# One list of weight buffers for two stages, a pinned entry to the second FFN, later transposes, and one block's token forms over five steps

## The chip, the cores and the metric

The kernel runs on one core of one Trainium2 chip. The metric is the device time of one execution in microseconds. The kernel before took 2645.22 us in the median of three runs (2639.3, 2645.22 and 2656.01 us). One more execution was recorded by the profiler: it took 2644.05 us, of which 2642.3 us lie between its first and its last instruction (the span). All times of the trace below are microseconds from the start of that span.

## The reference

One transformer layer on 256 latent tokens (LAT) and 256 context tokens (CTX) of width 2048, all in float32:

```
mod_l, mod_c = silu(c) @ w_mod + b_mod, silu(c_ctx) @ w_mod + b_mod      # shifts, scales, gates
xl = half_step_ffn(xl, mod_l, 0, ...);  xc = half_step_ffn(xc, mod_c, 0, ...)   # first FFN, 512 tokens
... token mixing: attention heads and mLSTM heads, one output projection ...
xl = half_step_ffn(xl, mod_l, 6, ...)                                    # second FFN, 256 tokens
return rms_norm(xl, g_final)

def half_step_ffn(x, mod, i, g, w_up, w_down):
    h = adaln(x, g, mod, i)
    a, b = split(h @ w_up, 2)                       # w_up 2048 x 2*5632, w_down 5632 x 2048
    return x + 0.5 * gate * ((silu(a) * b) @ w_down)
```

The inner width of 5632 is cut into 11 blocks of 512. The change lies in the two FFNs; what it touches of the rest is the buffer that every weight load passes through.

## The kernel before, in words

**Three products for one.** A float32 operand is split into a high and a low part of a format that TensorE multiplies fast: ScalarE (ACT) copies the weights into the high part and VectorE (DVE) subtracts to get the low part (`split`, L170 and L171, in halves of 1024 columns; `split_whole`, L140 and L141, 2048 columns at once). Each product is then three matmuls: high by high, low by high, high by low. `mm3` (L192 to L194) issues them in the order of its lines; `high_first` and `low_last` (L154, L155, L160) put the two that need only the high part of the weights first. The split halves live in two rings (`ringhi`, `ringlo`) of four places of 1024 columns, so that splitting can be about two halves-pairs ahead of TensorE (PE) and no further.

**Seven products for eight.** Both FFNs save matmuls by a Winograd-style scheme. Tokens and inner width are halved, four quarters a11, a12, a21, a22 of the tokens and four derived token forms (v, n1, s2, s4, s3) meet weights that are sums of four quarters of the weight block. One block of the first FFN's up product is `quad(n)` (L899): seven entries of `order` (L956), each with two steps q = 0 and 1, so 14 steps, numbered 2m + q. A step of the first FFN is 24 matmuls of 512 columns. The sums of weights are made by the DMA engines: a tile `chain_[q]` is loaded plain at the quad's start, used for a11, then a second quarter is added into it from memory by an accumulating DMA (`accum`, L784, issued by GpSimd (POOL)), used for n1, and so on through s2 and a22. So `chain_[q]` is read in steps 0, 4, 8 and 12 (q = 0) or 1, 5, 9, 13 (q = 1), with an accumulating DMA behind each of the first three reads. The entry a12 uses a plainly loaded tile (`plain`), and s4 and s3 share another one (`ra`, loaded by `loaded`, then accumulated into).

**Which tile holds what.** Plain loads go on the queue of SyncE (SP). `raw_tile()` (L118) takes a 128 x 2048 tile from a pool of three, tag `raw`; the pool hands out whichever of its three places has been given back. The two chain tiles are tiles of their own (L783). At the end of a quad `again(q)` (L939) loads the next quad's first quarter into the same chain tile (L817), so it must wait until the split of step 12 or 13 has read that tile, and it is read two steps later. The first FFN's down product has the same shape: `pair(p)` (L1106), five pairs of blocks, 14 steps each, `again(c)` at L1157 with the load at L1159. The second FFN has seven quads of its own (L2068, 14 steps of 12 matmuls), with chain tiles and an `again` of its own (L2110, load at L2113), and three blocks done plainly.

**Other work beside the quads.** While the quads of the first FFN run, the modulation vectors are summed on DVE, a half row at a time: a load of 512 KB (`sraw`, L292, two buffers, SP queue), then multiply and sum (L263). Each finished result `ca` of a quad (512 columns) waits in a list and is turned by four PE transposes (L893), copied by ACT into `stg` (one buffer, L883) and stored to memory (L884).

**Token forms of a down pair.** The seven token operands of a pair are made from the stored hidden tensors. What is made at which step stands in three tables: `first_plan` for the first pair (the entries from step 7 on are for the second pair), `plan` for the middle pairs and `last_plan` (L1078 to L1080). Each name is an instruction on DVE (`v`, `v2`, `u`, `u2`: one subtraction of 1.2 us) or a split to a place (`n1`, `s4`, `s2`, `s3`, `a22`, `a11`, `a12`: one copy on ACT, L768, and one subtraction on DVE, L769); `raw0` and `raw1` load the next hidden tensors (L759).

**What sets the order.** The framework's scheduler writes each engine's list of instructions ahead of time, from the program's order, the dependencies and a timing model of its own; at run time each engine goes through its list in order. `tc.keep_in_program_order` ties one instruction behind the instruction traced just before it on its engine; the token forms of the down pairs are tied in this way (`pinned`, `sub`, `neg_sub`), most others are not.

**The entry to the second FFN.** The last part of the first hidden block is L1951 to L1962: the product of two PSUM tiles (ACT Silu L1960, DVE multiply L1961) and the split of its result (L1932, L1933). Then the PSUM pools are closed and opened anew (L1966 to L1969), so the first matmuls of the next stage write into banks that L1961 reads. The main loop (L2253 to L2263) runs a plain block's up steps, the quads' steps and the down blocks' steps in turn, and steps the making of the four token forms (`token_forms`, L1998) after each of the first main steps.

**The transposes of the second FFN.** A finished hidden result goes on a list with the count of half-steps so far (`wait_turn`, L2061; `tiles` grows by 1 for a quad's step and by 2 for a step of a plain block). `turned` (L2037) transposes the first one on the list when the count has grown by 3. For a quad's second result the last elementwise steps are c21 (L2101): DVE add L2102, ACT Silu L2103, DVE multiply L2071 (`mul`).

Of the kernel before, what the change touches and what calls it, by code (L numbers as in the profile page):

```python
# [9 lines left out]
F32 = mybir.dt.float32  # L10
# [4 lines left out]
ALU = mybir.AluOpType  # L15
# [4 lines left out]
P = 128  # L20
# [28 lines left out]
FB = 4  # L49
# [12 lines left out]
def tile_layer(ctx: ExitStack, tc: tile.TileContext, I: dict, out: bass.AP):  # L62
# [74 lines left out]
    def split_whole(raw):  # L137

        hi, lo = ring(2)
        nc.scalar.activation(hi, raw, AF.Copy)  # L140
        nc.vector.tensor_tensor(lo, raw, hi.bitcast(F32), op=ALU.subtract)  # L141
        return lambda w: (hi[:, w], lo[:, w])

    def load_whole(src):
# [640 lines left out]
    with pool(name="f1u", bufs=1) as f1u:  # L785
# [27 lines left out]
        def part(n, ab, c):  # L813
            return I["w_up1b"][n - 1, ab, c]

        def first_chain(n, c):
            nc.sync.dma_start(chain_[c], part(n, 0, c))  # L817
# [81 lines left out]
        def quad(n, after=lambda step: None):  # L899
# [36 lines left out]
            def chained(ab, c):  # L936
                return lambda q: accum(chain_[q], part(n, ab, c + q))

            def again(q):  # L939
                if n + 1 < NB:  # L940
                    first_chain(n + 1, q)
                else:
                    nc.sync.dma_start(chain_[q], I["w_dn1"][0, 2 * q])

            def loaded(q):
                ra[q] = raw_tile()
                nc.sync.dma_start(ra[q], part(n, 1, 2 + q))
                return ra[q]

            def plain(q):  # L950
# [126 lines left out]

    first_plan = {0: "v n1", 1: "v2 u s4", 2: "s2 u2", 3: "s3 a22", 4: "raw0 raw1", 7: "a11", 8: "a12", 9: "v n1", 10: "v2 u", 11: "s4", 12: "s2 u2", 13: "s3"}  # L1078
    plan = {0: "a22 raw0", 1: "raw1", 4: "a11", 5: "a12", 6: "v", 7: "n1", 8: "v2 u", 9: "s4", 11: "s2 u2", 13: "s3"}
# [26 lines left out]
    def pair(p):  # L1106
# [44 lines left out]

        def loaded(m, cb):
            raw = raw_tile()
            nc.sync.dma_start(raw, w(m, cb))
            return raw

        def again(c):  # L1157
            if p + 1 < NP:
                nc.sync.dma_start(chain_[c], I["w_dn1"][2 * p + 2, 2 * c])  # L1159

        def b22(c):
            ra[c] = loaded(1, 2 * c + 1)
            return ra[c]
# [7 lines left out]
            ("a11", held, X, True, lambda c: accum(chain_[c], w(0, 2 * c + 1)), c11x),  # L1171
            ("a12", lambda c: loaded(1, 2 * c), Z, True, None, c11z),
# [3 lines left out]
            ("s3", lambda c: ra[c], X, False, None, x3),  # L1176
            ("a22", held, Y, True, again, c21),
        )
# [32 lines left out]
    for p in range(NP):  # L1211
        pair(p)

    def block_products(b, wt, t):
# [707 lines left out]
    with f2x:  # L1922
# [28 lines left out]
        for f in range(NPRE, FB):  # L1951
            pab = []
            for ab in range(2):
                wt = load_split(I["w_up2"][f, ab])
                b = bank()[:, :T]
                for k in range(KT):
                    mm3(b, *wt(slice(k * P, (k + 1) * P)), h2hi[:, k, :T], h2lo[:, k, :T], k == 0, k == KT - 1)
                pab.append(b)
            sa = sab_tile()[:, :T]
            nc.scalar.activation(sa, pab[0], AF.Silu)  # L1960
            nc.vector.tensor_tensor(sa, sa, pab[1], op=ALU.mult)  # L1961
            split_hid(hids[0], f, sa)  # L1962
        hscm.__exit__(None, None, None)
# [34 lines left out]
        def token_forms():  # L1998
# [8 lines left out]

            def difference(v, x, y):
# [10 lines left out]
            v, w = (acc2[:, t, 1024:].rearrange("p (k c) -> p k c", k=8) for t in range(2))  # L2019
            difference(v, a22, a21)  # L2020
            put(n1, v)
# [15 lines left out]
        def turned():  # L2037

            if not turn or turn[0][-1] + 3 > tiles[0]:
                return  # L2040
# [372 lines left out]
```

## Time and profile before

| what | value |
|---|---|
| profiled execution | 2644.05 us, span 2642.3 us, so 1.75 us outside the span |
| median of three runs | 2645.22 us (2639.3 to 2656.01) |
| first FFN: up quads, down pairs | about 144 to 949 us, about 949 to 1338 us |
| second FFN from its first plain block on | from 1982 us to the end |
| mean granted clock of TensorE | 0.996 |
| data moved | 679.94 MB, mean 257 GB/s |

In the profile, PE is TensorE's matmuls and transposes, PEld its weight loads, DVE is VectorE, ACT is ScalarE, POOL is GpSimd, SPq and POOLq are the instruction queues of SyncE and GpSimd, which here issue DMAs. A row of the timeline has the start and the length of one instruction (or of several merged, then xN), its engine, its line, the tile that it writes and the tiles that it reads, and in square brackets how long its engine sat idle before it and what ended that idle time. A row of the waits has the waiting engine and line, the engine and line that ended the wait, the total in microseconds, the number of such waits and the longest. A row of the windows has a stretch of time, its length, the busy time of each engine with the number of instructions, the granted clock of TensorE in that stretch (1.00 is full speed), the busy share of the 16 DMA engines and the rate in GB/s.

### The profile page before, as it was taken

Reading aid. Unit: us, or ns where it says so; the run is one execution under the profiler, and the core shown is the slowest. Engines: PE = TensorE matmul, PEld = TensorE weight load, DVE = VectorE, ACT = ScalarE, POOL = GpSimd, SP = SyncE. Lnnn points to the kernel's source line nnn. Section 1 sums busy time; section 2 is a strip of 40 time slices with the busy share of each in tenths; the row PEclk is TensorE's granted clock in tenths of the full one; section 3 lists DMA queues with packets and bytes.
Section 4 is the critical chain, followed back from the end, with each engine's and each line's share of the span. In section 5 each row is a group of like instructions: output and inputs, shape, how many; then the busy total and the mean of one; then the engine's idle time right before and its main releaser. Section 6 shows DMA issues by size and latency. Waiting matters only on the chain. (4 is left out here: it accounts for less than half of the span.)

```text
span 2642.3 us, 33359 instructions
## 1 busy us (share of the span) xinstructions
PE 2595.9 (98%) x12670; PEld 2148.3 (81%) x12670; DVE 2181.9 (83%) x2817; ACT 1345.2 (51%) x1547; POOL 210.7 (8%) x265
## 2 busy tenths in 40 slices
PE   8999999999999999999999999999999999999998
PEld 5787888888888878888889888877898888888887
DVE  6687888878878778888886979798598888887888
ACT  4354444544444455444454346346476555555554
POOL 0000001100000100010110000111000000000001
PEclk9999999999999999999999999999999999999999
DMA  9979999999999988889985867574568999889886
GB/s 376 343 229 259 257 283 269 271 285 280 271 280 268 276 230 237 221 208 230 231 244 215 315 227 246 207 271 159 175 253 262 294 273 295 259 271 307 285 244 188
DMA packets 136800, 679.94 MB, mean 257 GB/s; under 512 B 14392, under 2 KB 24376, under 8 KB 75840
## 3 DMA queue, kind: packets, MB, share of 16 engines
q1 hardware_dynamic: 108384, 496.92, 50.4%
q0 software_dynamic: 27968, 180.37, 34.8%
q8 instruction: 99, 1.62, 0.2%
q10 hardware_dynamic: 288, 0.52, 0.1%
q14 instruction: 61, 0.50, 0.1%
HBM read 658.82 MB, written 18.94 MB: 256 GB/s over the span
## 5 line engine op out<-in xcount | busy, mean ns | idle before, releaser
L170 ACT ACTIVATE ringhi<-raw 128x1024 fp32r<-128x1024 f32 (+4 forms) x363 | 370.6, 1025 | 429.0 <-PE mm L194 286.3
L171 DVE TENSOR_TENSOR ringlo<-raw,ringhi 128x1024 fp32r<-128x1024 f32 (+3 forms) x340 | 405.7, 1203 | 125.6 <-ACT ringhi L170 110.8
L192 PE MATMUL mm<-ringhi,hhi 128*128 128x512 f32 (+3 forms) x1024 | 391.0, 384 | 0.6 <-ACT ringhi L170 0.6
L193 PE MATMUL mm<-ringlo,hhi 128*128 128x512 f32 (+3 forms) x1024 | 387.5, 378 | 1.0 <-DVE ringlo L171 0.9
L194 PE MATMUL mm<-ringhi,hlo 128*128 128x512 f32 (+3 forms) x1024 | 387.2, 378 | 0.0
L170 ACT ACTIVATE ringhi<-chain 128x1024 fp32r<-128x1024 f32 x240 | 253.1, 1059 | 239.9 <-PE mm L194 143.3
L171 DVE TENSOR_TENSOR ringlo<-chain,ringhi 128x1024 fp32r<-128x1024 f32 x240 | 290.0, 1221 | 69.8 <-ACT ringhi L170 69.0
L263 DVE SCALAR_TENSOR_TENSOR junk<-sraw,cBh 128x1024 fp8e5<-128x1024 f32 x192 | 234.4, 1221 | 44.9 <-DMA sraw<-in_w_mt 42.6
L193 PEld LDWEIGHTS mm<-ringlo,hhi 128*128 128x128 f32 x1024 | 192.7, 188 | 33.5 <-DVE ringlo L171 2.6
L194 PEld LDWEIGHTS mm<-ringhi,hlo 128*128 128x128 f32 x1024 | 192.5, 188 | 33.4
L192 PEld LDWEIGHTS mm<-ringhi,hhi 128*128 128x128 f32 x1024 | 192.5, 188 | 31.7 <-ACT ringhi L170 0.8
L140 ACT ACTIVATE ringhi<-raw 128x2048 fp32r<-128x2048 f32 x78 | 149.7, 1920 | 129.3 <-PE mm L155 75.8
L141 DVE TENSOR_TENSOR ringlo<-raw,ringhi 128x2048 fp32r<-128x2048 f32 x78 | 178.6, 2289 | 39.1 <-ACT ringhi L140 37.6
L141 DVE TENSOR_TENSOR ringlo<-chain,ringhi 128x2048 fp32r<-128x2048 f32 x56 | 128.2, 2288 | 27.6 <-ACT ringhi L140 27.5
L140 ACT ACTIVATE ringhi<-chain 128x2048 fp32r<-128x2048 f32 x56 | 107.5, 1919 | 81.1 <-PE mm L155 26.9
L154 PE MATMUL mm<-ringhi,hid2h 128*128 128x512 f32 x320 | 124.7, 390 | 0.0
L155 PE MATMUL mm<-ringhi,hid2l 128*128 128x512 f32 x320 | 124.5, 389 | 0.0
L784 POOL DMA_DIRECT2D chain<-in_w_up1b x60 | 52.4, 873 | 651.5 <-DVE ringlo L171 543.1
L263 DVE SCALAR_TENSOR_TENSOR sr<-sr,cBl 128x1024 f32<-128x1024 f32 x72 | 87.1, 1215 | 7.2 <-DMA sr<-in_w_mt 7.1
L194 PE MATMUL mm<-hhi,ringlo 128*128 128x512 f32 (+1 forms) x256 | 87.9, 343 | 4.5 <-DVE ringlo L171 4.4
L192 PE MATMUL mm<-hhi,ringhi 128*128 128x512 f32 (+1 forms) x256 | 88.7, 347 | 0.0
L193 PE MATMUL mm<-hlo,ringhi 128*128 128x512 f32 (+1 forms) x256 | 87.0, 340 | 0.0
(513 smaller groups left out, 5940.2 us busy)
## 6 DMA issues: line engine op xcount, KB each, us to landing
raw<-in_w_dn SPq DMA_DIRECT2D x70, 1024.0 KB, 7.5
sraw<-in_w_mt SPq DMA_DIRECT2D x128, 512.0 KB, 7.7
chain<-in_w_up1b POOLq DMA_DIRECT2D x60, 1024.0 KB, 10.9
raw<-in_w_up1b SPq DMA_DIRECT2D x40, 1024.0 KB, 9.3
raw<-in_w_up2b SPq DMA_DIRECT2D x38, 1024.0 KB, 7.6
sr<-in_w_mt SPq DMA_DIRECT2D x69, 512.0 KB, 5.5
mraw<-in_w_m SPq DMA_DIRECT2D x32, 1024.0 KB, 9.2
chain<-in_w_dn POOLq DMA_DIRECT2D x30, 1024.0 KB, 8.5
```

The lines of the kernel that those rows point to most:

```text
L140: nc.scalar.activation(hi, raw, AF.Copy)
L141: nc.vector.tensor_tensor(lo, raw, hi.bitcast(F32), op=ALU.subtract)
L154: nc.tensor.matmul(out_ap, sh, mh, start=first, stop=False, skip_group_check=True)
L155: nc.tensor.matmul(out_ap, sl, mh, start=False, stop=False, skip_group_check=True)
L170: nc.scalar.activation(hi, src, AF.Copy)
L171: vector[0].tensor_tensor(lo, src, hi.bitcast(F32), op=ALU.subtract)
L192: tensor[0].matmul(out_ap, sh, mh, start=first, stop=False, skip_group_check=skip)
L193: tensor[0].matmul(out_ap, sh, ml, start=False, stop=False, skip_group_check=skip)
L194: tensor[0].matmul(out_ap, sl, mh, start=False, stop=last, skip_group_check=skip)
L263: ins = nc.vector.scalar_tensor_tensor(junk() if junk else raw, raw, 1.0, cB[s], op0=ALU.mult, op1=ALU.mult, accum_out=mT[:, i, s, kt, h : ...
L784: accum = lambda dst, src: nc.gpsimd.dma_start(dst, src, accum_op=ALU.add)
```

## The change

Four things are changed; the number of matmuls, the bytes loaded and the arithmetic stay as they were.

1. **The list.** The pool of three raw tiles becomes three lasting tiles in a list `free`; `take` pops the first, `give` puts one at the end, and `raw_tile()` does both at once. In the quads of the first FFN and in its down pairs the two chain tiles join this list: the next first quarter is loaded into a tile taken from the list behind step 8 (q = 0) and behind step 10 (q = 1, just after the list got back the `ra` tile of q = 0), and at steps 12 and 13 the old chain tile goes to the list and the new one takes its role. In a down pair both next tiles are taken in steps 10 and 11.
2. **The entry.** The split of the last part of the first hidden block is traced after the first step of the plain block instead of before it, and two DVE instructions are tied into program order: the low part of the first `split_whole` of the second FFN, and the first subtraction of the first token form.
3. **The transposes.** For a quad's second result (sign below 0, t = 1) the count must have grown by 4 instead of 3, so its four transposes move behind one more step.
4. **The table.** `first_plan` spreads the token forms of the first down pair over steps 0 to 4 instead of 0 to 3. (`s4` moves from step 1 to 2, `u2` from 2 to 3, `a22` and the two loads go to step 4.)

```diff
+    free = [wp.tile([P, 2048], F32, name=f"raw{i}", bufs=1) for i in range(3)]
+    lasting = list(free)
+    def take():
+        return free.pop(0)
+    def give(t):
+        free.append(t)
     def raw_tile(n=2048):
-        t = wp.tile([P, 2048], F32, tag="raw", name="raw", bufs=3)
+        t = take()
+        give(t)
...
-        nc.vector.tensor_tensor(lo, raw, hi.bitcast(F32), op=ALU.subtract)
+        low = nc.vector.tensor_tensor(lo, raw, hi.bitcast(F32), op=ALU.subtract)
+        if in_order:
+            in_order.pop()
+            tc.keep_in_program_order(low)
...
-            def again(q):
-                if n + 1 < NB:
-                    first_chain(n + 1, q)
-                else:
-                    nc.sync.dma_start(chain_[q], I["w_dn1"][0, 2 * q])
+            def ahead(q):
+                following[q] = take()
+                nc.sync.dma_start(following[q], part(n + 1, 0, q) if n + 1 < NB else I["w_dn1"][0, 2 * q])
+            def after_s2(q):
+                chained(0, 2)(q)
+                if not q:
+                    ahead(0)
+            def after_s3(q):
+                give(ra[q])
+                if not q:
+                    ahead(1)
+            def passed(q):
+                give(chain_[q])
+                chain_[q] = following[q]
             def loaded(q):
-                ra[q] = raw_tile()
+                ra[q] = take()
...
-                (s2, held, X, False, chained(0, 2), c12),
-                (s3, lambda q: ra[q], X, False, None, c22),
-                (a22, held, Y, True, again, c21),
+                (s2, held, X, False, after_s2, c12),
+                (s3, lambda q: ra[q], X, False, after_s3, c22),
+                (a22, held, Y, True, passed, c21),
...
-    first_plan = {0: "v n1", 1: "v2 u s4", 2: "s2 u2", 3: "s3 a22", 4: "raw0 raw1", 7: "a11", ...
+    first_plan = {0: "v n1", 1: "v2 u", 2: "s4 s2", 3: "u2 s3", 4: "a22 raw0 raw1", 7: "a11", ...
...
-        def again(c):
+        def next_first(c):
             if p + 1 < NP:
-                nc.sync.dma_start(chain_[c], I["w_dn1"][2 * p + 2, 2 * c])
+                following[c] = take()
+                nc.sync.dma_start(following[c], I["w_dn1"][2 * p + 2, 2 * c])
+            give(ra[c])
+        def passed(c):
+            give(chain_[c])
+            chain_[c] = following.get(c)
...
-            split_hid(hids[0], f, sa)
+            if f < FB - 1:
+                split_hid(hids[0], f, sa)
+        in_order.append(True)
...
-                sub(v, h1, h2)
+                ins = sub(v, h1, h2)
+                if in_turn:
+                    tc.keep_in_program_order(ins)
...
-            if not turn or turn[0][-1] + 3 > tiles[0]:
+            if not turn or turn[0][-1] + 3 + (turn[0][3] < 0 and turn[0][1]) > tiles[0]:
...
                 next(main)
+                if sa is not None:
+                    split_hid(hids[0], FB - 1, sa)
+                    sa = None
                 tiles[0] += 2
```

More of the change, by code (lines that the diff above doesn't have):

```diff
@@ L1150, in c21, with loaded @@
             through_gate(2 * s + 1, 2 * c)
-        def loaded(m, cb):
-            raw = raw_tile()
+        def loaded(m, cb, raw):
             nc.sync.dma_start(raw, w(m, cb))
             return raw
-        def again(c):
+        following = {}
+        def next_first(c):
             if p + 1 < NP:
-                nc.sync.dma_start(chain_[c], I["w_dn1"][2 * p + 2, 2 * c])
+                following[c] = take()
[4 more added lines that the diff above has]
+            chain_[c] = following.get(c)
         def b22(c):
-            ra[c] = loaded(1, 2 * c + 1)
+            ra[c] = loaded(1, 2 * c + 1, take())
             return ra[c]
@@ L1171, in pair @@
             ("a11", held, X, True, lambda c: accum(chain_[c], w(0, 2 * c + 1)), c11x),
-            ("a12", lambda c: loaded(1, 2 * c), Z, True, None, c11z),
+            ("a12", lambda c: loaded(1, 2 * c, raw_tile()), Z, True, None, c11z),
             ("n1", held, Y, True, lambda c: accum(chain_[c], w(1, 2 * c + 1)), p5),
@@ L1175, in pair @@
             ("s2", held, X, False, lambda c: accum(chain_[c], w(1, 2 * c)), c12),
-            ("s3", lambda c: ra[c], X, False, None, x3),
-            ("a22", held, Y, True, again, c21),
+            ("s3", lambda c: ra[c], X, False, next_first, x3),
+            ("a22", held, Y, True, passed, c21),
         )
@@ L1212, in tile_layer @@
         pair(p)
+    free[:] = [t for t in free if any(t is x for x in lasting)]
+    assert len(free) == len(lasting)
     def block_products(b, wt, t):
@@ L2019, in token_forms @@
             v, w = (acc2[:, t, 1024:].rearrange("p (k c) -> p k c", k=8) for t in range(2))
-            difference(v, a22, a21)
+            difference(v, a22, a21, True)
             put(n1, v)
```

6 lines of the change are left out of this document (4 added, 2 removed).

## The prediction

> **What bounds the kernel now.** First the busy times and the span, then the stretches by granted clock and DMA share, then what PE waited for.
>
> ```profile
> span 2642.3 us, 33359 instructions
> PE 2595.9 (98%) x12670; PEld 2148.3 (81%) x12670; DVE 2181.9 (83%) x2817; ACT 1345.2 (51%) x1547; POOL 210.7 (8%) x265
> q1 hardware_dynamic: 108384, 496.92, 50.4%
> ```
>
> TensorE is the bound: it is idle for 2642.3 - 2595.9 = 46.4 us in all, and the change removes no matmul. So a gain can only come from those 46.4 us and from stretches in which matmuls run slowly. A gain of over 1% (26 us) would need more than half of it. A difference of 1% is also about what a measurement of this kernel can tell from none, since the three runs shown lie 17 us apart.
>
> ```profile
> 210.00:220.00 10.00, 8.70 (x30) 6.84 (x31) 8.61 (x9) 5.45 (x6) 0.86 (x1) 0.83 0.98 191
> 400.00:450.00 50.00, 48.71 (x217) 39.78 (x217) 40.76 (x53) 26.67 (x31) 5.20 (x6) 1.00 1.01 263
> 960.00:970.00 10.00, 7.80 (x34) 5.79 (x33) 10.00 (x10) 8.73 (x10) 0.00 (x0) 1.00 0.31 108
> 970.00:980.00 10.00, 10.00 (x39) 8.04 (x38) 8.48 (x9) 2.61 (x3) 0.86 (x1) 0.83 0.88 320
> 1982.00:2004.00 22.00, 21.64 (x95) 17.94 (x96) 19.85 (x16) 10.60 (x8) 0.94 (x1) 1.00 0.81 297
> ```
>
> Two things stand here. In the first FFN's quads the DMA engines are as good as full (1.01), so a load that is issued earlier can only displace others. And after some stalls the granted clock falls: 0.83 over 970 to 980 means 0.17 x 10 = 1.7 us lost on top of the idle time; the same at 210 to 220.
>
> How long a step is: eight matmuls of 512 columns take 1.98 us with the last one's 0.39 in it, so one each (1.98 - 0.39) / 7 = 0.227 us. A step of the first FFN (24) is 5.45 us, one of the second FFN's quads (12) 2.73 us.
>
> ```profile
> 2168.10 1.98 PE L160 MATMUL mm<-ringlo,hid2h 128*128 128x512 f32 x8
> L155 PE MATMUL mm<-ringhi,hid2l 128*128 128x512 f32 x320 | 124.5, 389 | 0.0
> ```
>
> **Part 1, the list.** The next chain load is issued when the last split has read the tile, two steps before it is needed:
>
> ```profile
> 783.54 0.34 SPq L817 DMA_DIRECT2D chain<-in_w_up1b  x1
> 791.59 1.06 ACT L170 ACTIVATE ringhi<-chain 128x1024 fp32r<-128x1024 f32 x1 [5.73 <-DMA chain<-in_w_up1b]
> 792.68 1.23 DVE L171 TENSOR_TENSOR ringlo<-chain,ringhi 128x1024 fp32r<-128x1024 f32 x1 [2.68 <-ACT ringhi L170]
> 794.66 0.52 PE L893 MATMUL tr<-ident,ca 128*128 128x128 f32 x3 [1.79 <-DVE ca L897]
> 399.88 2.01 ACT L170 ACTIVATE ringhi<-chain 128x1024 fp32r<-128x1024 f32 x2 [1.27 <-DMA chain<-in_w_up1b]
> 404.32 0.50 PE L193 MATMUL mm<-ringlo,hhi 128*128 128x512 f32 x1 [0.90 <-DVE ringlo L171]
> ```
>
> At 783.54 the load is issued, at 791.59 ACT goes on after 5.73 us of waiting; Silu and multiply of the finished quad stand behind that split in ACT's and DVE's lists, and PE pays 1.79 us. At 404 the same costs 0.90. Following the list by hand through ten quads, the next tile for q = 0 has been free for 11 steps when its first quarter is needed, and every other load (q = 1, `plain`, `ra`) for 5 to 7. Five steps are 27 us, splitting runs a step or two ahead, so 16 us are left, against landings of 6.5 to 11 us (rows below). These two PE waits should go: 0.90 + 1.79 = **2.7 us**. The ten loads for the down pairs (two at the quads' end, eight in pairs) hide already: no PE wait of size there names a plainly loaded chain. 0.
>
> ```profile
> sraw<-in_w_mt SPq DMA_DIRECT2D x128, 512.0 KB, 7.7
> chain<-in_w_up1b POOLq DMA_DIRECT2D x60, 1024.0 KB, 10.9
> chain<-in_w_up1b SPq DMA_DIRECT2D x20, 1024.0 KB, 6.5
> SPq L817 <- DVE ringlo L171: 36.0, 17, 4.0
> ```
>
> What it may cost: SP's list is in order, and each of the 17 chain loads of the quads made SP wait for a split, 4.0 us at most. After the change the one for q = 0 needn't wait and the one for q = 1 waits for step 10's split instead of step 13's; behind it stand `sraw` loads and `stg` stores. And in full DMA engines a moved megabyte delays others: 50.4% of 2642.3 us for 496.92 MB is 2.7 us per MB. An accumulating load has four steps (21.8 us) less a step or two of early splitting, so some 13 us, for its 10.9: 2 to 3 us of cover, about one such load. `sraw` is the weakest place, see the rivals. I take 0; the bounds of the whole part are -18 (rival (d)) and 2.7.
>
> [...]
>
> Outside the two stages `raw_tile` hands out the three tiles in turn; the pool handed out whichever was free, which for loads that are read in the order of their issue is the same tile. 0.
>
> **Part 2, the entry.** The first matmul of the plain block waits for L1961 to free its bank:
>
> ```profile
> 1979.60 2.28 DVE L141 TENSOR_TENSOR ringlo<-raw,ringhi 128x2048 fp32r<-128x2048 f32 x1
> 1981.81 0.41 DVE L1961 TENSOR_TENSOR sab<-sab,mm 128x256 f32<-128x256 f32 x1
> 1980.26 0.28 PE L194 MATMUL mm<-h2hi,ringlo 128*128 128x256 f32 x1
> 1982.36 0.47 PE L154 MATMUL mm<-ringhi,h2hi 128*128 128x512 f32 x1 [1.82 <-DVE sab L1961]
> ```
>
> The product is complete at 1980.26 + 0.28 = 1980.54, but DVE is inside `ringlo` until 1981.81. With `ringlo` tied behind, L1961 runs at 1980.54 to 1980.95, and with the 0.14 us seen between its end (2.22) and PE's start (2.36) PE starts at 1981.1: **1.3 us** gained. Then `ringlo` ends at 1983.2; PE needs it after 16 high matmuls, 3.6 us, at 1984.7: covered by 1.5 us. Price: three subtractions of the first token form (1.2 us each) no longer fit in before the entry, so DVE gets 3.5 us more in 1982 to 2004, where it has 22 - 19.85 = 2.2 us idle; the low parts there run a step ahead. Bounds -1.3 (what doesn't fit) and 1.82.
>
> **Part 3, the transposes.** In the second FFN a quad's last result is late in the same way, at four of seven quads, and that FFN's chain is not changed:
>
> ```profile
> PE tr L2049 <- DVE ca L2071: 3.8, 4, 1.3
> 2166.38 1.92 ACT L140 ACTIVATE ringhi<-chain 128x2048 fp32r<-128x2048 f32 x1 [3.41 <-DMA chain<-in_w_up2b]
> 2170.53 0.69 DVE L2071 TENSOR_TENSOR ca<-ca,cy 128x512 f32<-128x512 f32 x1
> 2171.36 0.63 PE L2049 MATMUL tr<-ident,ca 128*128 128x128 f32 x4 [1.29 <-DVE ca L2071]
> ```
>
> One more step in between gives 2.73 us, more than the longest wait of 1.3, and that step's first high part (2166.38 + 1.92 = 2168.30) is there before PE asks. **3.8 us**; bounds 0 (other work takes the place of the wait) and 3.8. The hidden block is first read three steps (8.2 us) after the old place; 5.5 us are left for a copy and a subtraction.
>
> **Part 4, the table.** At the first down pair DVE is full (10.00 of 10):
>
> ```profile
> 964.54 1.22 DVE L1051 TENSOR_TENSOR hidh<-hidh 128x1024 f32<-128x1024 f32 x1
> 965.68 1.22 DVE L769 TENSOR_TENSOR sumshh<-hidl,sumshh 128x1024 fp32r<-128x1024 f32 x1
> 967.41 2.35 DVE L171 TENSOR_TENSOR ringlo<-raw,ringhi 128x1024 fp32r<-128x1024 f32 x2
> 962.41 0.50 PE L193 MATMUL mm<-ringlo,hidl 128*128 128x512 f32 x1 [0.30 <-DVE ringlo L171]
> 968.68 0.50 PE L193 MATMUL tr<-ringlo,hidl 128*128 128x512 f32 x1 [1.90 <-DVE ringlo L171]
> 972.66 0.33 SPq L759 DMA_DIRECT2D hidl<-hid  x1
> 988.21 1.05 ACT L768 ACTIVATE sumshh<-hidh 128x1024 fp32r<-128x1024 f32 x1
> ```
>
> The low part of a12's second tile (967.41) stands behind `u2` (964.54) and `s4` (965.68). `u2` moves to step 3, behind that low part: 1.14 us earlier. `s4` and `s2` stay ahead of step 3 and may stay in front. So the stall shrinks from 1.90 to about 0.8, and the slow clock after it (1.7) should go: the idle time of 1.82 us above was followed by full clock, 1.00 in 1982 to 2004. **2.8 us**; bounds 0 and 0.30 + 1.90 + 1.7 = 3.9. `a22` falls into step 4; the hidden loads come 5.45 us later than 972.66, land some 9 us after that, at 987, and ACT first reads them at 988.21: covered by 1 us.
>
> [...]
>
> **Sum.** 2.7 + 1.3 + 3.8 + 2.8 = 10.6 us. Against the profiled execution, 2644.05 - 10.6 = 2633.4 us; that execution is 1.2 us under the median of the runs shown, so the same forecast for a median is 2634.6. I say 2634.
>
> **Rivals.** The rows for them:
>
> ```profile
> 210.54 0.50 PE L192 MATMUL mm<-ringhi,s2h 128*128 128x512 f32 x1 [1.14 <-ACT ringhi L170]
> 211.80 0.50 PE L193 MATMUL mm<-ringlo,s2h 128*128 128x512 f32 x1 [0.76 <-DVE ringlo L171]
> DVE junk L263 <- DMA sraw<-in_w_mt: 42.6, 23, 3.3
> 448.99 0.50 PE L193 MATMUL mm<-ringlo,s2h 128*128 128x512 f32 x1 [0.39 <-DVE ringlo L171]
> 957.60 1.23 DVE L171 TENSOR_TENSOR ringlo<-raw,ringhi 128x1024 fp32r<-128x1024 f32 x1 [3.58 <-ACT ringhi L170]
> ```
>
> (a) *The table does nothing*: ACT's list, not DVE's, is what is late there, so the 1.90 us and the slow clock stay: 2634 + 2.8 = 2637. For it: before 957.60 DVE sits idle for 3.58 us, waiting for ACT. Against it: DVE then works without a pause up to the stall. (b) *The stall at 210 goes too*, as SP's list becomes another one: 1.14 + 0.76 + 1.7 = 3.6 us more, 2630. Against it: nothing in the change aims there. (c) *The waits only move*: the lists are written anew from a timing model, and stalls of 1 to 2 us appear elsewhere for those that go: 2644. For it: the idle time of now is made of such stalls. Against it: a load that lands steps ahead leaves nothing to wait for. (d) *Slower*: early chain loads hold up `sraw`. DVE already waits for it 23 times, 42.6 us, and is in order, so low parts behind it come late (448.99: 0.39 us of PE). An `sraw` has two buffers and 13 loads in 76 us, so 11.7 us from issue to need, against 7.7: 4 us of cover. It decides from the point where two moved megabytes (5.4 us) go ahead of one `sraw`. With one more DVE wait as long as the longest (3.3) in each of nine quads, of which PE pays 2 us: + 18, without part 1's 2.7: 2634 + 20.7 = 2655.
>
> **Chances.** Forecast 0.42, (a) 0.18, (b) 0.12, (c) 0.16, (d) 0.12. The range runs from 2622 (all bounds at their best, (b), and a run 6 us under the median as one of those shown) to 2650 ((c) and 6 us above); (d) and what is beyond are left out. Faster by over 1% (under 2619) no case gives: 0.04 for what I don't see. Slower by over 1% (over 2671) needs (d) at nearly twice its price: 0.05. Within 1%: 0.91.
>
> **What would show it.** Right: no PE wait at a quad's first steps and ACT no longer waiting for plain chain loads in the first FFN; L1961 ahead of `ringlo`; no PE wait on L2071; clock 1.00 after the first down pair's start. Wrong: a longer wait of L263 for `sraw`, PE idle time of over 40 us again, or a new stall where low parts stand behind the token forms after the entry.

## The result, and the profile after

| what | before | after |
|---|---|---|
| median of the runs | 2645.57 us (9 runs, 2638.21 to 2656.01) | 2632.34 us (9 runs, 2626.66 to 2634.63) |
| profiled execution, its span | 2644.05 us, 2642.3 us | 2632.74 us, 2631.0 us |

The ratio after to before is 0.9948, with a 95% interval of 0.9934 to 0.9962: 13.2 us less in the medians, 10 to 17 us by the interval. That is half a per cent, inside the 1% of the prediction's main case, and the interval excludes zero. The forecast of 2634 us lies 1.7 us above the median. The profiled executions differ by 11.3 us in their spans.

First the page of the changed kernel: its span, its engines and its SP queue.

```profile
span 2631.0 us, 33355 instructions
...
PE 2590.5 (98%) x12670; PEld 2144.2 (81%) x12670; DVE 2181.8 (83%) x2817; ACT 1345.4 (51%) x1547; POOL 210.2 (8%) x265
...
q1 hardware_dynamic: 108384, 496.92, 50.6%
```

The count of matmuls and the bytes are the same. TensorE's idle time fell from 46.4 to 2631.0 - 2590.5 = 40.5 us, which is 5.9 of the 11.3. The other 5.4 is busy time, 2595.9 - 2590.5: the same matmuls ran less often at a lower clock (a mean of 0.998 in place of 0.996). Nearly all of it is three stretches of slow clock behind stalls, from 212.4, 970.2 and 1642.6 us on in the profile before, each with a granted clock of 0.50 for 3.41 us, so 1.7 us; the profile after has none behind the opening (1.00 from 60.2 us to the last matmul). Only the one at 970 lies where the change was made.

The stretches in which the prediction saw stalls or slow clock, in the changed kernel (start and end, length, busy time of PE, PEld, DVE, ACT and POOL, granted clock, DMA share, GB/s):

```profile
960.00:970.00 10.00, 9.37 (x41) 7.10 (x40) 10.00 (x12) 7.98 (x9) 0.00 (x0) 1.00 0.52 191
970.00:980.00 10.00, 10.00 (x44) 8.26 (x45) 7.00 (x7) 5.23 (x7) 2.60 (x3) 1.00 0.98 274
1974.00:1996.00 22.00, 22.00 (x97) 18.22 (x98) 21.90 (x17) 11.04 (x8) 0.94 (x1) 1.00 0.86 303
210.00:220.00 10.00, 10.00 (x48) 8.30 (x47) 8.00 (x9) 4.07 (x5) 0.86 (x1) 1.00 1.03 236
```

The clock is 1.00 in all four. DVE is full after the entry, 21.90 of 22 us, and PE loses nothing by it (22.00 of 22 us busy). And what TensorE still waits for that bears on the change, over the whole span:

```profile
PE mm L208 <- DVE ringlo L186: 1.4, 2, 1.0
...
PE mm L169 <- DVE sab L1999: 0.7, 1, 0.7
```

(L208 is the low part's matmul of `mm3`, L193 before; L1999 is the multiply of the entry, L1961 before.) The waits on `ca` at the quads' starts and at the second FFN's transposes have no row any more.

Where the time went, read from the starts of the same PE instruction in both traces (after less before, differences of the profiled pair):

| place | us |
|---|---|
| opening, before the first FFN | +2.6 |
| around 210 us | -4.1 |
| quads: around 404 and 449, around 794 | -2.2 and -2.0 |
| quads: elsewhere, among it a new stall near 900 | +1.8 |
| first down pair | -3.0 |
| entry | -1.2 |
| transposes of the second FFN | -3.8 |
| the rest, among it +1.7 near 1500 and -1.3 near 1640 | +0.6 |

The list, the first down pair, the entry and the transposes make 10.4 together, close to the forecast's 10.6. But 4.1 lies at 210 us, where nothing was changed, 2.6 was given back in the opening, and the rest holds two more such items. Since one pair of profiles has such items of chance in it, the experiments look at each part in several kernels.

### The profile page after: what moved, and what is told of

The parts are those of the page before. It is cut to its first block, busy times and chain, and to the rows that moved or that the text cites. A ratio compares the mean times of both kernels' runs of the same rounds, so it can differ in the third digit from the quotient of the medians.

```text
span 2631.0 us, 33355 instructions
## 1 busy us (share of the span) xinstructions
PE 2590.5 (98%) x12670; PEld 2144.2 (81%) x12670; DVE 2181.8 (83%) x2817; ACT 1345.4 (51%) x1547; POOL 210.2 (8%) x265
## 3 DMA queue, kind: packets, MB, share of 16 engines
q1 hardware_dynamic: 108384, 496.92, 50.6%
## 5 line engine op out<-in xcount | busy, mean ns | idle before, releaser
L185 ACT ACTIVATE ringhi<-raw 128x1024 fp32r<-128x1024 f32 (+4 forms) x433 | 444.9, 1031 | 504.1 <-PE mm L209 341.9
L186 DVE TENSOR_TENSOR ringlo<-raw,ringhi 128x1024 fp32r<-128x1024 f32 (+3 forms) x410 | 491.1, 1208 | 137.6 <-ACT ringhi L185 123.3
L208 PE MATMUL mm<-ringlo,hhi 128*128 128x512 f32 (+3 forms) x1024 | 387.1, 378 | 0.4 <-DVE ringlo L186 0.3
L278 DVE SCALAR_TENSOR_TENSOR junk<-sraw,cBh 128x1024 fp8e5<-128x1024 f32 x192 | 234.6, 1222 | 51.8 <-DMA sraw<-in_w_mt 49.4
L185 ACT ACTIVATE ringhi<-chain 128x1024 fp32r<-128x1024 f32 x170 | 179.9, 1060 | 160.4 <-PE mm L209 117.6
L186 DVE TENSOR_TENSOR ringlo<-chain,ringhi 128x1024 fp32r<-128x1024 f32 x170 | 205.6, 1222 | 45.0 <-ACT ringhi L185 43.4
L208 PEld LDWEIGHTS mm<-ringlo,hhi 128*128 128x128 f32 x1024 | 192.7, 188 | 32.5 <-DVE ringlo L186 1.7
L208 PE MATMUL mm<-hlo,ringhi 128*128 128x512 f32 (+1 forms) x256 | 86.3, 337 | 0.0
L175 PE MATMUL mm<-ringlo,hid2h 128*128 128x512 f32 x320 | 79.3, 389 | 0.0
```

The lines of the kernel that those rows point to most:

```text
L175: nc.tensor.matmul(out_ap, sh, ml, start=False, stop=last, skip_group_check=True)
L185: nc.scalar.activation(hi, src, AF.Copy)
L186: vector[0].tensor_tensor(lo, src, hi.bitcast(F32), op=ALU.subtract)
L208: tensor[0].matmul(out_ap, sh, ml, start=False, stop=False, skip_group_check=skip)
L278: ins = nc.vector.scalar_tensor_tensor(junk() if junk else raw, raw, 1.0, cB[s], op0=ALU.mult, op1=ALU.mult, accum_out=mT[:, i, s, kt, h : ...
```

## The experiments

The parts are called the list, the entry, the transposes and the table, as in the prediction. Each kernel's name stands in brackets beside what was measured; before and after are the two kernels of the profiles above.

**The parts alone.** The list without the other three:

```diff
 (the changed kernel, with)
-    first_plan = {0: "v n1", 1: "v2 u", 2: "s4 s2", 3: "u2 s3", 4: "a22 raw0 raw1", ...
+    first_plan = {0: "v n1", 1: "v2 u s4", 2: "s2 u2", 3: "s3 a22", 4: "raw0 raw1", ...
-            if f < FB - 1:
-                split_hid(hids[0], f, sa)
-        in_order.append(True)
+            split_hid(hids[0], f, sa)
...
-            if not turn or turn[0][-1] + 3 + (turn[0][3] < 0 and turn[0][1]) > tiles[0]:
+            if not turn or turn[0][-1] + 3 > tiles[0]:
```

> Only the list of tiles; the entry, the transposes and the table are as before. Theory (early chain loads): the PE waits at about 404 us (0.90) and 794 us (1.79) before a quad's first steps and transposes are gone, the stalls at the first down pair (0.30 and 1.90), at the entry (1.82) and on L2071 (3.8 in all) stay; 2.7 to 4 us faster than before, ratio about 0.9987. Rival (the list also removes the stall near 210 us, because SP's list of instructions is another one): 3.6 us more, 6 to 8 us faster, ratio about 0.9973, and no stall near 210 us. Rival (waits only move): ratio 1.000 with new stalls of 1 us in the quads.

Measured (list_only): 2639.06 us, ratio 0.9968 [0.9953, 0.9984], so 8.5 us less (4 to 12; the medians differ by 6.4). The window over the quads, from 230 us, where all first loads are done, to 935:

```profile
230.00:935.00 705.00, 704.74 (x3175) 582.16 (x3174) 591.43 (x759) 347.10 (x400) 62.76 (x72) 1.00 0.99 275
```

TensorE is idle for 0.26 us of 705. The waits at 404 and 794 us are gone and the stalls of the other three parts stay, as expected, but the gain is above the 2.7 to 4 us expected and nearer to the rival's 6 to 8. The rival's reason doesn't hold: the stall near 210 us is absent here, but also in the next two kernels, which leave the quads as they were. Then the table alone, in the kernel before:

```diff
-    first_plan = {0: "v n1", 1: "v2 u s4", 2: "s2 u2", 3: "s3 a22", 4: "raw0 raw1", ...
+    first_plan = {0: "v n1", 1: "v2 u", 2: "s4 s2", 3: "u2 s3", 4: "a22 raw0 raw1", ...
```

> Only the table first_plan; all else as before. Theory: the wait of 1.90 us at a12's second tile shrinks to 0.6 to 0.8 us and the clock after it stays at 1.00; 2.8 us faster, ratio about 0.9989; the stalls at 404 and 794 us stay as before. Rival (what fell in the changed kernel fell by the list, which relieves the DMA engines around the first down pair): wait of about 1.9 us stays, ratio 1.000. The quads of the first FFN are untouched here: if the stall near 210 us is absent in this run too, it comes and goes with the run and is no work of the list.

Measured (table_only): 2641.07 us, 0.9984 [0.9971, 0.9997], 4 us less (1 to 8). In the trace the stall of a12's second tile is 0.62 us in place of 1.90, with a clock of 1.00 in the 10 us behind it. The entry and the transposes alone, in the kernel before:

```diff
+        if in_order:
+            in_order.pop()
+            tc.keep_in_program_order(low)
...
-            split_hid(hids[0], f, sa)
+            if f < FB - 1:
+                split_hid(hids[0], f, sa)
+        in_order.append(True)
...
-            if not turn or turn[0][-1] + 3 > tiles[0]:
+            if not turn or turn[0][-1] + 3 + (turn[0][3] < 0 and turn[0][1]) > tiles[0]:
```

> Only the entry to the second FFN and the later transposes; all else as before. Theory: the entry's wait goes from 1.82 to about 0.7 us and the four waits on L2071 (3.8 us) go; 4.9 to 5.4 us faster, ratio about 0.9980. Rival (the waits return one step later or at the token forms' first readers): under 2 us faster, ratio about 0.9995. The quads of the first FFN are untouched: stalls at 404 and 794 us as before, and the one near 210 us if it belongs to the instruction lists.

Measured (entry_transposes): 2639.29 us, 0.9979 [0.996, 0.9998], 6 us less (0.5 to 11). All of the waits on `ca` at the transposes are gone. And the changed kernel with the old table:

```diff
-    first_plan = {0: "v n1", 1: "v2 u", 2: "s4 s2", 3: "u2 s3", 4: "a22 raw0 raw1", ...
+    first_plan = {0: "v n1", 1: "v2 u s4", 2: "s2 u2", 3: "s3 a22", 4: "raw0 raw1", ...
```

> The changed kernel with the table first_plan of before. Theory: parts add up, so 2.8 us less gain than the changed kernel: ratio about 0.9959 against 0.9948, and a wait of 1 to 2 us at the first down pair. Rival (the table matters only together with the old list): the first down pair shows the same 0.6 us wait as the changed kernel and the ratio is 0.9948.

Measured (old_table): 2634.67 us, 0.9951 [0.9933, 0.997]. The wait of 1.90 us is back, as expected; the ratio lies between the two that were expected and tells neither from the other. What follows: the list is the largest part. The product of the three ratios is 0.9931, against 0.9948 [0.9934, 0.9962] for the whole; with intervals this wide that is no contradiction, and no sign that one part lives on another. The table is worth 0.0016 alone and 0.0003 on top of the rest; only the first of the two differs from nothing by its interval.

**What of the list does it.** The list changes two things: which tile a raw load gets, and where the next quarter goes. The kernel before with the first alone, three lasting tiles handed out in turn while the chain is reloaded in place:

```diff
+    free = [wp.tile([P, 2048], F32, name=f"raw{i}", bufs=1) for i in range(3)]
     def raw_tile(n=2048):
-        t = wp.tile([P, 2048], F32, tag="raw", name="raw", bufs=3)
+        t = free.pop(0)
+        free.append(t)
```

> The kernel before with the three raw tiles as lasting tiles handed out in turn; the chain loads still go into the tile just read, at the old place. Theory (what helps is that the next chain load has a tile that was freed steps ago): nothing changes, 3 to 5 us of PE idle time in the quads of the first FFN stay and the ratio is 0.9995 to 1.0005. Rival (lasting tiles instead of a pool change the lists, and that is the gain): idle time in the quads under 1.3 us and a ratio of 0.997 to 0.998, as for the list alone.

And the kernel before itself, profiled once more beside it:

> The kernel before once more, for a second profile. Theory: the stalls in the first FFN's quads that hang on a chain load's landing (near 404 and 794 us) come at varying places from run to run, with 3 to 5 us of PE idle time in the quads in every run, and the stall near 210 us (3.6 us with the slow clock) is a matter of the single run and may be absent. Rival (the lists fix these stalls): PE waits at the same places and of the same length within 0.3 us, the one near 210 us among them.

Measured: 2645.13 us, 1.0 [0.9984, 1.0017] (same_tile), and 2642.18 us in the single run of the kernel before (before_again). The quads' window and the waits of ACT on chain loads in it, of the kernel with the lasting tiles:

```profile
230.00:935.00 705.00, 696.64 (x3118) 573.95 (x3117) 579.62 (x740) 339.05 (x391) 62.62 (x72) 1.00 0.98 270
```

```profile
ACT ringhi L173 <- DMA chain<-in_w_up1b: 19.5, 10, 7.8
```

The lasting tiles alone leave the time as it was, the waits (ten of them, up to 7.8 us) and TensorE's idle time, 8.36 us in this profile, well above the 3 to 5 expected. The same window of the kernel before, in the profile of the prediction and in the new one:

```profile
230.00:935.00 705.00, 701.75 (x3158) 578.73 (x3157) 585.16 (x747) 343.89 (x396) 62.77 (x72) 1.00 0.98 274
```

```profile
230.00:935.00 705.00, 700.62 (x3147) 578.73 (x3147) 587.11 (x751) 343.87 (x395) 62.62 (x72) 1.00 0.98 273
```

So the same code is idle for 3.25 us in one run and 4.38 in another. The two large stalls are at the same two instructions in both, with other lengths: 1.10 us at 399 and 2.76 at 791 in the new one, 0.90 at 404 and 1.79 at 794 in the old. The new one has another of 0.52 at 709.5, and none near 210. Neither what was expected (varying places) nor the rival (the same lengths within 0.3 us) describes this. Next, the changed kernel with the two loads written where the old ones stood, at steps 12 and 13, but still into a free tile:

```diff
             def after_s2(q):
                 chained(0, 2)(q)
-                if not q:
-                    ahead(0)
             def after_s3(q):
                 give(ra[q])
-                if not q:
-                    ahead(1)
             def passed(q):
+                ahead(q)
                 give(chain_[q])
                 chain_[q] = following[q]
```

> The changed kernel with both next chain loads of the up quads written at steps 12 and 13, where they stood before, but into a tile of the list that was freed 2 to 9 steps earlier. Theory (it is the free tile that counts; the scheduler moves a load without dependencies up by itself): as the changed kernel, PE idle time in the quads of the first FFN 0 to 1.4 us, chain loads issued 5 steps and more ahead, ratio 0.994 to 0.996. Rival (the place in the program decides when the load is issued): idle time of 3 to 5 us and the waits near 400, 710 and 790 us back, ratio 0.996 to 0.998.

It ran beside the changed kernel, taken again:

> The changed kernel once more, beside the next one. Theory: ratio 0.9935 to 0.996, PE idle time in the quads 0 to 1.4 us, waits of 0.63 us at the first down pair and 0.68 us at the entry, both followed by full clock; the stalls of DVE behind its 512 KB loads fall at other places than in the first profile of it.

Measured: 2631.81 us, 0.9951 [0.9933, 0.9968] (late_load), beside 2631.8 us, 0.9954 [0.9938, 0.997] (after_again): no difference. TensorE's idle time in the quads is 1.18 and 1.87 us, the second above the 1.4 expected; the waits of after_again at the first down pair and the entry, 0.62 and 0.68 us, are followed by full clock (1.00 in the 10 us behind each), as expected. The two issues of next chain loads ahead of the quad that begins near 790 us, in the kernel with the late lines, in the changed kernel and in the kernel before:

```profile
719.20 0.33 SPq L958 DMA_DIRECT2D chain<-in_w_up1b  x1
...
757.78 0.33 SPq L958 DMA_DIRECT2D chain<-in_w_up1b  x1
```

```profile
722.35 0.33 SPq L958 DMA_DIRECT2D chain<-in_w_up1b  x1
...
760.93 0.33 SPq L958 DMA_DIRECT2D chain<-in_w_up1b  x1
```

```profile
776.62 0.33 SPq L817 DMA_DIRECT2D chain<-in_w_up1b  x1
```

In the kernel before the second of the two is the load at 783.54 that the prediction shows. The quad's first transposes start at 786.14, 789.29 and 794.66 us in the three; counted from there, the last load is issued 28.4 us ahead with the list, written early or late, and 11.1 us ahead in the kernel before. So the line's place in the program is not what sets the issue: the scheduler brings the load forward to where its tile is free. The free tile is the part of the list that works; the steps at which the loads are written are not.

**Whether moved megabytes hurt.** Rival (d) lived on DMA engines that are as good as full. The changed kernel with one more megabyte per quad, copied from memory to memory on SP's queue behind the first of the next chain loads:

```diff
             def ahead(q):
                 following[q] = take()
                 nc.sync.dma_start(following[q], part(n + 1, 0, q) if n + 1 < NB else I["w_dn1"][0, 2 * q])
+                if not q:
+                    tc.keep_in_program_order(nc.sync.dma_start(dr.tile([P, 2048], F32, name=f"extra{n}"), part(n, 0, 0)))
```

> The changed kernel with one more megabyte moved in each of the ten quads of the first FFN, from memory to memory, behind the next chain load on the same queue; nothing waits for it. Theory (DMA engines as good as full, share of 1.01): each adds 2.7 us or more of DMA time that nothing hides, DVE waits longer for its 512 KB loads, and the kernel is 15 to 40 us slower than the changed one (ratio to before about 1.000 to 1.010). Rival (the share counts packets that wait, and there is room): under 4 us slower than the changed one, ratio to before 0.994 to 0.9965.

Measured (extra_mb): 2643.45 us, 0.9984 [0.997, 0.9998]: against the changed kernel's 2632.34 us some 11 us for ten extra megabytes (9.5 by the two ratios), about 1 us each. Neither number expected was right; it lies between them. The worst place in its trace, on PE and on DVE, and its DVE waits for `sraw` over the whole span:

```profile
438.31 0.70 PE L208 MATMUL mm<-ringlo,s4h 128*128 128x512 f32 x1 [3.72 <-DVE ringlo L186]
```

```profile
434.61 1.23 DVE L278 SCALAR_TENSOR_TENSOR junk<-sraw,cBh 128x1024 fp8e5<-128x1024 f32 x1 [4.68 <-DMA sraw<-in_w_mt]
...
437.03 2.35 DVE L186 TENSOR_TENSOR ringlo<-raw,ringhi 128x1024 fp32r<-128x1024 f32 x2
```

```profile
DVE junk L278 <- DMA sraw<-in_w_mt: 58.0, 24, 4.9
```

DVE waits 4.68 us for an `sraw`, the low part stands behind it, and TensorE pays 3.72 us, with a slow clock behind: its next matmul takes 0.63 us in place of 0.39. That is rival (d)'s mechanism, step for step. In the quads' 705 us TensorE is idle for 6.34 us here; where the rest of the 11 us lies stays open. In the changed kernel it is there too, small, near 900 us:

```profile
896.11 1.23 DVE L278 SCALAR_TENSOR_TENSOR junk<-sraw,cBh 128x1024 fp8e5<-128x1024 f32 x1 [3.46 <-DMA sraw<-in_w_mt]
...
898.53 2.35 DVE L186 TENSOR_TENSOR ringlo<-chain,ringhi 128x1024 fp32r<-128x1024 f32 x2
```

```profile
899.80 0.50 PE L208 MATMUL mm<-ringlo,s4h 128*128 128x512 f32 x1 [1.02 <-DVE ringlo L186]
```

**A sixth step for the table.** The 0.63 us that is left at a12's second tile invited a table over six steps:

```diff
-    first_plan = {0: "v n1", 1: "v2 u", 2: "s4 s2", 3: "u2 s3", 4: "a22 raw0 raw1", ...
+    first_plan = {0: "v n1", 1: "v2 u", 2: "s4", 3: "s2 u2", 4: "s3 raw0", 5: "a22 raw1", ...
```

> The changed kernel with the token forms of the first down pair over six steps (s2 and u2 in step 3, s3 in step 4, a22 in step 5; the first hidden load stays in step 4, the second goes to step 5). Theory (DVE's order of work at that place is the whole of the stall): the wait of 0.63 us at a12's second tile goes to under 0.2, no later stall; 0.5 us faster than the changed kernel, too little to measure, ratio to before 0.9946. Rival (the later hidden loads or s2 come too late): a wait of 1 to 3 us between 975 and 995 us and ratio 0.995 to 0.996.

Measured (six_table): 2630.73 us, 0.9936 [0.9919, 0.9953]; the stall is gone in the trace. It was run once more, on the same chip as the changed kernel:

> The changed kernel with the token forms over six steps, beside the changed kernel on the same chip. Theory: 0.6 us of 2632, so no difference that these runs can tell (0.05%); ratios within 0.001 of each other. Rival (the stall of 0.63 us starts something larger in some runs, such as a slow clock): 2 us or more faster than the changed kernel.

Measured (six_again): 2633.92 us, 0.9957 [0.994, 0.9974], beside 0.9954 [0.9938, 0.997] for the changed kernel. The six steps beat the kernel before and can't be told from the five. The first run by itself would have passed for a gain of 1.6 us.

## Why the prediction was right, and where it was not

**Bound and size: right.** TensorE's idle time and its slow clock are where all of the gain lies (5.9 and 5.4 of the 11.3 us between the profiled executions), no matmul less. The sum of 10.6 us stands against 13.2 [10, 17].

**The list: the right mechanism, a term too small.** The term of 2.7 us was read from one profile, of a kernel whose stalls vary in size, and in part in place, from run to run. The idle time of TensorE in the 705 us of the quads, over all profiles but the one with added megabytes:

| next quarter goes | kernel: idle time, us | mean |
|---|---|---|
| into the same chain tile | before 3.25, before_again 4.38, same_tile 8.36, table_only 3.13, entry_transposes 4.77 | 4.8 |
| into a free tile | list_only 0.26, old_table 0.00, after 1.23, after_again 1.87, late_load 1.18, six_table 1.39, six_again 0.58 | 0.9 |

All five of the first row lie above all seven of the second. The list's idle time is 4.8 - 0.9 = 3.9 us (2.9 without same_tile, whose 8.36 weighs most). To this comes a term that the prediction lacked: a slow clock behind the longest of these stalls, 2.76 us in before_again and 3.76 in same_tile.

```profile
790.27:793.68 3.41, 3.06 (x10) 2.62 (x11) 3.41 (x5) 1.23 (x2) 0.89 (x1) 0.50 0.49 180
```

```profile
793.05:796.46 3.41, 2.62 (x9) 2.27 (x10) 3.41 (x6) 1.48 (x3) 0.63 (x1) 0.50 0.57 181
796.46:799.88 3.42, 3.42 (x10) 2.65 (x9) 3.16 (x5) 1.06 (x1) 0.26 (x1) 0.50 0.99 165
```

By the clock in the 10 us behind each (0.85 and 0.70) that is 1.5 and 3.0 us in two of five profiles, 0.9 in the mean, and none in the seven of the second row. So the term is 4.8 us, inside the timed 4 to 12 (3.3 without same_tile). What may lie beyond it, up to the timed 8.5, has no place in the traces.

The cost was taken as 0, with a bound of -18. SP's waits ahead of the chain loads became longer, in the changed kernel:

```profile
SPq L958 <- DVE ringlo L186: 80.7, 20, 8.1
```

80.7 us in place of 36.0, while TensorE's idle time in the quads fell from 3.25 to 1.23 us: SP's longer waits ahead of loads that are early cost nothing here that shows. DVE's wait for `sraw` was named as the sign of a wrong prediction: 49.4 us in the changed kernel, above the 42.6 of before. But list_only shows 38.4, after_again 41.7 and same_tile 46.5, so this total does not follow the list. The real price is the 1.02 us at 899.80, and what else stands in the second row of the table. The extra megabytes tell why rival (d) did not come: at about 1 us of time per added megabyte its price was real, but the list only moves its loads earlier, and adds none. So the premise that in DMA engines with a share of 1.01 an earlier load can only displace others did not hold: the two chain loads shown above came 49 and 17 us earlier in their quad, and TensorE waited less. The prediction's 2.7 us per megabyte was the time of the DMA engines; about a third of it reached the end. With the extra megabytes on SP's queue the accumulating loads into the chain tiles, which GpSimd issues, landed in 12.2 us in the median, in place of 11.0 in the changed kernel, and the `sraw` loads in 8.2 in place of 7.7.

**The entry: right in its order, wrong in the clock behind it, and worth more.** DVE and PE at the entry of the changed kernel:

```profile
1973.43 0.42 DVE L1999 TENSOR_TENSOR sab<-sab,mm 128x256 f32<-128x256 f32 x1 [2.36 <-PE mm L209]
1973.77 2.28 DVE L151 TENSOR_TENSOR ringlo<-raw,ringhi 128x2048 fp32r<-128x2048 f32 x1
```

```profile
1973.05 0.28 PE L209 MATMUL mm<-h2hi,ringlo 128*128 128x256 f32 x1
1974.00 0.47 PE L169 MATMUL mm<-ringhi,h2hi 128*128 128x512 f32 x1 [0.68 <-DVE sab L1999]
```

The multiply goes ahead of the low part, and the wait is 0.68 us in place of 1.82: 1.14 us, where 1.3 was predicted. What is left is the chain from the product to the multiply to the bank. The full DVE behind it costs PE nothing. The step that failed is the one on the clock: "the idle time of 1.82 us above was followed by full clock". That was the exception. The granted clock in the 10 us after the same stall, in the kernel before profiled again and with the table alone:

```profile
1978.67:1988.67 10.00, 10.00 (x38) 8.20 (x39) 9.68 (x8) 3.39 (x4) 0.00 (x0) 0.86 0.93 360
```

```profile
1978.30:1988.30 10.00, 10.00 (x37) 8.09 (x38) 9.48 (x8) 3.98 (x4) 0.00 (x0) 0.83 0.93 358
```

The old entry's stall (1.82, 2.50, 2.40, 1.85 and 1.83 us in five profiles) is followed by a slow clock in four of the five. With the new entry it is 0.67 or 0.68 in eight, and the clock is 1.00 each time. So the entry is worth 2.08 - 0.68 = 1.4 us of idle time and 4/5 of 1.7 us: 2.8.

**The transposes: right, with a wait that comes back at times.** No wait on `ca` is left in the second FFN, in any of the eight profiles with the new rule; the five with the old one have 3.2 to 4.3 us of it, 3.6 in the mean, against 3.8 predicted. The multiply and the transposes at the first place where PE had waited 1.29 us:

```profile
2162.23 0.68 DVE L2113 TENSOR_TENSOR ca<-ca,cy 128x512 f32<-128x512 f32 x1
```

```profile
2164.28 0.60 PE L2091 MATMUL tr<-ident,ca 128*128 128x128 f32 x4
```

The result is ready at 2162.91 and is wanted at 2164.28. But in four of the eight, 15 to 20 us later, PE waits for ACT, which waits for a plain load: 1.02, 1.57, 1.29 and 1.48 us. The four others have none there and at most 0.38 at a like place near 2430, and the five with the old rule have neither beyond 0.15. The mean over the eight is 0.8, so the part nets about 2.9. That the lost stall had been hiding this late load is likely, but was not tried.

**The table: the stall right, the clock too dear.** DVE at the first down pair of the changed kernel:

```profile
958.87 1.22 DVE L186 TENSOR_TENSOR ringlo<-raw,ringhi 128x1024 fp32r<-128x1024 f32 x1
960.09 1.23 DVE L784 TENSOR_TENSOR sumshh<-hidl,sumshh 128x1024 fp32r<-128x1024 f32 x1
...
962.96 1.22 DVE L186 TENSOR_TENSOR ringlo<-raw,ringhi 128x1024 fp32r<-128x1024 f32 x1
...
964.70 1.22 DVE L1080 TENSOR_TENSOR hidh<-hidh 128x1024 f32<-128x1024 f32 x1
```

```profile
964.24 0.50 PE L208 MATMUL tr<-ringlo,hidl 128*128 128x512 f32 x1 [0.63 <-DVE ringlo L186]
```

`u2` (964.70) stands behind a12's low part (962.96), `s4` (960.09) stayed in front, and PE waits 0.63 us at 964.24 where about 0.8 was predicted. The hidden loads are read late enough and cost nothing, as predicted. Their cover was larger than the 1 us of the prediction, which set the load of `hidl` against the first read of `hidh`: in the kernel before `hidl` is first read at 993.65. The slow clock of 1.7 us was charged in full. That is the second step that failed. With the old table, two kernels with the same stall:

```profile
959.91:969.91 10.00, 10.00 (x37) 8.11 (x38) 8.62 (x9) 3.14 (x4) 0.62 (x1) 0.83 0.77 302
```

```profile
960.59:970.59 10.00, 10.00 (x44) 8.30 (x45) 9.69 (x10) 3.88 (x6) 0.86 (x1) 1.00 0.76 279
```

The first is the list alone (1.89 us of idle time), the second the changed kernel with the old table (1.90 us). Of six stalls of 1.80 to 1.90 us at this place, two were followed by slow clock. So the term is 1.9 - 0.6 = 1.3 us and a third of 1.7: 1.8, not 2.8. Rival (a) is out: two thirds of the stall do go.

**The new sum.** 4.8 + 2.8 + 2.9 + 1.8 = 12.3 us (10.8 with 3.3 for the list), inside the measured 10 to 17. The 10.6 came out close because two terms were too small (the list by 2.1 at most, the entry by 1.5) and two too large (the transposes by 0.9, the table by 1.0). That these errors nearly cancel is luck.

**The other rivals.** (b) seemed to come true, -4.1 us at 210. It is not work of the change: of thirteen profiles only that of the prediction has this stall; the kernel before, profiled again, does not. (c) held in two small places, the 1.02 us at 899.80 and the load after the transposes. As for the slow clock, stalls of 1.80 to 2.50 us at the entry and the first down pair were followed by it in six of eleven cases. So in these traces a stall of this length had a slow clock behind it at times, not each time.

## What to carry to other kernels

Where a buffer is reloaded in place, the load waits for its last reader; a free buffer took that wait away here (the load went out 28.4 us ahead in place of 11.1), and the program line where the load is written mattered less than the buffer being free. Stalls in such a loop come, go and change size from run to run (1.79 and 2.76 us at the same instruction in two profiles of the same kernel), so a term read from one profile may be off by half: profile the unchanged kernel a second time, and look at the whole stage's idle time rather than at named stalls. A slow clock behind a stall of about 2 us should be entered with the share of cases in which it was seen (here six of eleven), not as a fixed price, and the share should come from several profiles.

## What the runs showed of the hardware

**The clock.** The granted clock in the 10 us after idle times of almost the same length differs: at the entry 1.82 us was followed by 1.00 (before) and 1.83 us by 0.83 (list_only); at the first down pair 1.89 us was followed by 0.83 (list_only), and 1.90 by 0.83 (before) and by 1.00 (old_table). Stalls of 0.61 to 0.68 us at these two places were followed by 1.00 each time. In the kernel before, each of the three slow stretches between the opening and the last matmul has a clock of 0.50 for 3.41 us, which makes the 1.7 us of above. A stall of 2.29 us near 1640 us, which the change does not touch, is in both profiled executions: in the kernel before it ends at 1641.58 us and the 10 us behind it have a clock of 0.83, in the changed kernel it ends at 1635.48 us and they have 1.00. So in these traces the length of a stall alone does not tell whether a slow clock follows, and what else decides stays open.

**The DMA engines.** In the quads, where the DMA share is 0.98 to 0.99, ten added megabytes cost about 11 us. By 2.7 us each it would have been 27; by the share of their queue (51.2% of 2641.5 us against 50.6% of 2631.0) they took some 21 us of the engines' time. Over the 705 us the rate rose from 276 to 284 GB/s at the same share of 0.99: this share still left room for 8 GB/s more.

Why one store of a hidden tensor's piece was slow at 210 us in a single run (ACT waited 6.55 us for it) stays open as well.
